# Attention: the last key quarter projected later, and two output-projection chunks between its transposed keys and its scores

## Chip, core and metric

One core of one Trainium2 chip. The metric is device time in microseconds. The kernel before took 1267.77 us (median of 3 runs, 1267.5 to 1268.72).

## What is computed

Two layers over 256 latent tokens (with a 256-token context in layer 0), each a half-step SwiGLU, a mixer and another half-step SwiGLU, with DeepNorm residuals. Layer 0's mixer is the neighbourhood attention that the change touches:

```
qkv = (hx @ w_qkv).reshape(B, S, 3, N_HEADS, HEAD_DIM)      # 16 heads of 64
q, k = apply_axial_rope(q), apply_axial_rope(k); v = qkv[:, :, 2]
s_win = einsum(q_rows, k_blk) * scale + bias   (window mask: -inf)
s_ctx = einsum(q_rows, k_c) * scale            (all 256 context keys)
p = softmax(concatenate([s_win, s_ctx]))
o = p_win @ v_blk + p_ctx @ v_c
y_lat = o.reshape(B, S, D) @ w_out
```

## The kernel before, in words

Everything is done in float32 accuracy by splitting each operand into a high and a low half: ScalarE (ACT) copies the high half, VectorE (DVE) subtracts to get the low half, and TensorE (PE) adds three products (`mmu`, L156: lines L160, L161 and L163, six matmuls of 128x512 for one *chunk*, that is one weight unit of two 128-row blocks against one token tile).

The attention stage works on these pieces.

- **Key quarters.** `kv_quarter(g)` (L879) projects keys and values of heads 4g to 4g+3: 16 chunks named wkv (4 token tiles by 4 weight units, `tile_panel`, L863). For each finished tile, `each` turns the keys (rope on DVE for the latent tiles; a plain copy on ACT, L887, for the two context tiles) and splits the values. Its `rest` (L895) is put off (`Late`): eight transposes in two groups of four write two PSUM banks named kT, from which ACT and DVE make kTh and kTl (L108, L109).
- **Query halves.** `q_half` (L908), 8 chunks wq and a late qT of the same kind.
- **Score pairs.** `scores(h, qt)` (L931): six matmuls S (L941) into two PSUM banks for the heads h and h+1 and one half of the queries. Then on DVE the bias is added (L945) and the maximum is taken (L947); on ACT the exponential (L949) reads the bank, and L951 scales it to the probabilities `pr`. There are 16 pairs in 32 steps.
- **Transposed probabilities.** `probs_T` (L960): four transposes into a bank PT, split into pTh on ACT and pTl on DVE. `values(h)` (L971): eight matmuls o, then osum on ACT (L984) and DVE (L985), and after two heads the split oT.
- **Output projection.** `last_filler` (L1007) loads the residual x and the gate and makes the chunks wo of `na_w_out` in the order of `order_late` (L494): three banks (t, n) = (0,0), (0,1), (1,0) first.
- **Bias.** `bias_pair` (L847) loads four small pieces per pair on the SP queue, POOL adds the window mask (L857). Four bias tiles serve two pairs, so that a pair's load waits until the pair two before it has added its own.

The PSUM has eight banks, `PB = {"mm": 3, "at": 3, "tp": 2}`. All transposes (PT, kT, qT, hT and the small mcT of `fold_cols`, L341) take the two tp banks in turn (`tpb`, L104). Score pairs take at banks, chunks and o take mm banks (`mmb`, L101), but a wo bank with t = 1 is an at bank too.

PE's order is the order of the Python program; ACT, DVE, SP and POOL are ordered by a scheduler with priorities. The loop of L1033 to L1060 sets PE's order: at step i it places the score pair (even i), some chunks of a generator `fill`, the PT of step i-2 and the o of step i-3. How many chunks a step gets is `rate`: R0 for steps 0 to 7, R1 for 8 to 15, R2 for 16 to 23 and R3 after that. `fill` yields key quarters 1 and 2, query half 1 and key quarter 3 (L1001). A `while` (L1038) makes chunks in addition until the quarter that step i + AHEAD will read is complete. From step 24 on (L1048) `fill` is the output projection, of which the loop may use 9 chunks.

Of the kernel before, what the change touches and what calls it, by code (L numbers as in the profile page):

```python
# [20 lines left out]
NH = 16  # L21
# [21 lines left out]
NX_AT = 2  # L43
R0 = 2.4
R1 = 2.9
R2 = 1.9
R3 = 1.0
LN_LAG = (5, 5)
LT_LAG = (5, 5)
F0_LAG = (5, 5, 6, 7)  # L50
# [1 line left out]
ROPE_EARLY = 70  # L52
S_EARLY = 40
V_LAG = 1
AHEAD = 3
P_EARLY = 70
V_EARLY = 70
W_HI = 2
# [8 lines left out]
def backbone_kernel(  # L67
# [27 lines left out]
    def act(dt=F32, s="a"):  # L95
        return ap.tile([P, 512], dt, tag="act", name=nm(s))

    def bank(tag, s):
        return pp.tile([P, 512], F32, tag=tag, bufs=PB[tag], name=nm(s))

    def mmb(s="mm", t=0):  # L101
        return bank("at" if t % 2 else "mm", s)

    def tpb(s="tp"):  # L104
        return bank("tp", s)

    def split(src, hi, lo):
        a = nc.scalar.activation(hi, src, AF.Copy)  # L108
        return a, nc.vector.tensor_tensor(out=lo, in0=src, in1=hi.bitcast(F32), op=ALU.subtract)  # L109
# [344 lines left out]
    def run(gen):  # L454
        for _ in gen:
            pass
# [37 lines left out]
    def order_late(nu, halved=False):  # L494


        e = nu - 1
        banks = ((0, 0), (0, 1), (1, 0))
        o = [(t, n, u) for t, n in banks for u in range(e - 1)] + [(t, n, e - 1) for t, n in banks]
        if halved:  # L500
            o += [(t, n, (e, i)) for i in range(UK) for t, n in banks]
        else:
            o += [(t, n, e) for t, n in banks]
        return o + [(1, 1, u) for u in range(nu)]
# [167 lines left out]
    steps = ((0, 1), (1, 1), (2, 2), (4, 2), (6, 2))  # L672
# [80 lines left out]
    def new_x(l, i, pool=None):  # L753
        lnr = ln_rows(l, i, pool)
        for t in range(2):
            for h in range(2):
                nc.vector.tensor_tensor(out=xt[t][h], in0=xt[t][h], in1=lnr[0][h], op=ALU.mult)
                nc.vector.tensor_tensor(out=xt[t][h], in0=xt[t][h], in1=lnr[1][h], op=ALU.add)
# [35 lines left out]
    def lhs_T(tl):  # L794
        def f(k, t):
            s = (k % 2) * 256 + t * P
            g = tl[k // 2]
            hi, lo = g.get() if isinstance(g, Late) else g
            return hi[:, s:s + P], lo[:, s:s + P]
        return f  # L800
# [23 lines left out]
    def rtile(n):  # L824
        if n == 256:
            return hp.tile([P, n], F32, tag="kr", bufs=8, name=nm("kr"))
        return sp.tile([P, n], F32, tag="s2", bufs=S2, name=nm("qr"))

    def roped(src, t, which, nh):
        n = nh * HD  # L830
        C = rope[:, t, 2 * which, :]
        S = rope[:, t, 2 * which + 1, :].rearrange("p (a b e) -> p a b e", a=2, b=2)
        r1 = rtile(n)
        r2 = sp.tile([P, n], F32, tag="tmp", bufs=3, name=nm("r2"))
        nc.vector.tensor_tensor(out=r1.rearrange("p (h d) -> p h d", h=nh), in0=src.rearrange("p (h d) -> p h d", h=nh),
                                in1=C.unsqueeze(1).to_broadcast([P, nh, HD]), op=ALU.mult)
        bv = src.rearrange("p (h a b e) -> p h a b e", h=nh, a=2, b=2)
        rv = r2.rearrange("p (h a b e) -> p h a b e", h=nh, a=2, b=2)
        for b in range(2):
            nc.vector.tensor_tensor(out=rv[:, :, :, b, :], in0=bv[:, :, :, 1 - b, :],  # L840
                                    in1=S[:, :, b, :].unsqueeze(1).to_broadcast([P, nh, 2, 16]), op=ALU.mult)
        nc.vector.tensor_tensor(out=r1, in0=r1, in1=r2, op=ALU.add)
        return r1
# [19 lines left out]
    def tile_panel(c0, c1, hl, s, each):  # L863

        units = []
        for t, hT in enumerate(hl):
            bk = mmb(s)
            for u in range(KU):
                if t == 0:
                    units.append(wpair(w_qkv, u, c0, c1, s))  # L870
                hi, lo = units[u]
                mmu(bk, [(*hsl(hT, UK * u + i), hi[:, i], lo[:, i]) for i in range(UK)], u == 0, u == KU - 1)
                if u == KU - 1:
                    with tc.high_priority(offset=ROPE_EARLY):
                        each(t, bk)
                yield
                tick()

    def kv_quarter(g, res):  # L879
        krs, v = [], []  # L880

        def each(t, bk):
            if t < 2:
                krs.append(roped(bk[:, 0:256], t, 1, 4))
            else:
                r1 = rtile(256)
                nc.scalar.activation(r1, bk[:, 0:256], AF.Copy)  # L887
                krs.append(r1)
            v.append(act(F32R, "v"))
            z = v[t].rearrange("p (h s d) -> p h s d", h=4, s=2)  # L890
            split(bk[:, 256:512].rearrange("p (h d) -> p h d", h=4), z[:, :, 0], z[:, :, 1])

        yield from tile_panel(D + g * 256, 2 * D + g * 256, [hTs[t] for t in range(4)], "wkv", each)

        def rest():  # L895
            kT = []
            for j in range(2):
                ps = tpb("kT")
                for t in range(4):
                    nc.tensor.transpose(ps[:, t * P:(t + 1) * P], krs[t][:, j * P:(j + 1) * P], ident)  # L900
                hi, lo = act(F32R, "kTh"), act(F32R, "kTl")
                split(ps, hi, lo)
                kT.append((hi, lo))
            return kT

        res.append((Late(1, rest), v))
# [22 lines left out]
    KV, Q = [], []  # L929
# [71 lines left out]
    def filler():  # L1001
        yield from kv_quarter(1, KV)
        yield from kv_quarter(2, KV)
        yield from q_half(1, Q)
        yield from kv_quarter(3, KV)

    def last_filler():  # L1007
        with tc.issue_after(bias_dma[-1].ins):
            for t in range(2):
                for h in range(2):  # L1010
                    xt[t][h] = act(F32, "x")
                    sync.dma_start(xt[t][h], xscr[t * P:(t + 1) * P, h * 512:(h + 1) * 512])
            gen, nh, lt = sub_end(na_w_out[0], lhs_T(oT), KC, 0, 1, 5, 1.0, (0, 6), "wo", order_late(KU, True))
        box.extend([nh, lt])
        yield from gen

    box = []
    fill = filler()
    rate = [R0] * 8 + [R1] * 8 + [R2] * 8 + [R3] * 12
    credit = 0.0  # L1020
    steps = [(h + i, qt) for h in range(0, NH, 2) for qt in range(2) for i in range(2)]
    prs = {}
    LAG = A_LAG
    fin = None

    def fill_some(n):
        for _ in range(n):
            if next(fill, 0) == 0:
                break

    fill_some(A_PRE)
    for i in range(len(steps) + LAG + V_LAG):
        if i == NX_AT:  # L1033
            new_x(0, 0, s2t)
            for t in range(2):
                for h in range(2):
                    sync.dma_start(xscr[t * P:(t + 1) * P, h * 512:(h + 1) * 512], xt[t][h])
        while i + AHEAD < len(steps) and len(KV) <= steps[i + AHEAD][0] // 4:  # L1038
            fill_some(1)
        if i < len(steps) and i % 2 == 0:  # L1040
            with tc.high_priority(offset=S_EARLY):
                prs[i], prs[i + 1] = scores(*steps[i])
            if i % 2 == 0 and i + 2 < len(steps):
                bias_pair(*steps[i + 2])
        credit += rate[min(i, len(rate) - 1)]
        n = int(credit)
        credit -= n
        if i >= 24 and fin is None:  # L1048
            run(fill)
            fin = last_filler()  # L1050
            fill = islice(fin, 10)
        fill_some((n + 1) // 2)
        if i == len(steps) + LAG - 1:
            run(fill)
        if 0 <= i - LAG < len(steps):
            with tc.high_priority(offset=P_EARLY):
                probs_T(*steps[i - LAG], prs.pop(i - LAG))
        fill_some(n // 2)
        j = i - LAG - V_LAG
        if j >= 0 and steps[j][1] == 1:  # L1060
            with tc.high_priority(offset=V_EARLY):
                values(steps[j][0])
# [80 lines left out]
    g, hTs, later = sub_end(sc_w_out[0], lhs_T(yT), KC, 1, 1, 5, 1.0, (1, 6), "wo", order_late(KU))  # L1143
# [57 lines left out]
```

## Time and profile before

| | |
|---|---|
| median of 3 runs | 1267.77 us |
| the profiled execution | 1267.5 us |
| its span, first to last instruction | 1265.7 us |
| mean granted TensorE clock | 0.998 |
| PE busy | 1241.6 us |
| DVE busy | 955.1 us |
| ACT busy | 591.4 us |

The span is the time from the first to the last instruction of the profiled execution; 1.8 us lie around it. An idle time of an engine is put down to what released it, in brackets behind the instruction that ended it. A busy PE says only that matmuls were in flight: they overlap, so the spacing between starts is the better measure of what a matmul costs.

### The profile page before, as it was taken

To read this page: it belongs to the slowest core of one execution; us is meant where nothing else is said; L and a number is where in the kernel's file an instruction comes from. 1 tells how busy PE (TensorE), PEld (TensorE's weight loads), DVE (VectorE), ACT (ScalarE), POOL (GpSimd) and SP (SyncE) were. 2 spreads that over 40 slices of the span, in tenths; PEclk is the share of its full clock that TensorE was granted. 3 is DMA by queue.
4 is the path that set the end of the run, shared out by engine and by line. 5 is a ranking of instruction groups with operands and counts; after the bars stand their busy time and mean duration, and the time that the engine had idled before them with its cause. 6 is when DMAs were issued, how large, how long until landed. Compare 5 with 4: busy or idle time off the path is not lost.

```text
span 1265.7 us, 17259 instructions
## 1 busy us (share of the span) xinstructions
PE 1241.6 (98%) x5890; PEld 1004.0 (79%) x5890; DVE 955.1 (75%) x1685; ACT 591.4 (47%) x1152; POOL 41.6 (3%) x71
## 2 busy tenths in 40 slices
PE   6999999999999999999999999999999999999997
PEld 4787778787778878777888788888788887888786
DVE  4698987588888867889888646988546788877546
ACT  2433132312326556687655535655435644655431
POOL 0000000000001111111000000000000000000000
PEclk9999999999999999999999999999999999999999
DMA  9977679597872744464899745898645764886641
GB/s 283 299 243 233 179 235 300 168 304 232 294 237 84 209 100 86 99 135 135 261 323 335 233 145 175 268 330 278 223 149 168 238 211 134 257 288 186 218 159 57
DMA packets 202776, 268.59 MB, mean 212 GB/s; under 512 B 30090, under 2 KB 149362, under 8 KB 202688
## 3 DMA queue, kind: packets, MB, share of 16 engines
q1 hardware_dynamic: 202652, 267.48, 67.4%
q8 instruction: 46, 0.75, 0.2%
q14 instruction: 42, 0.34, 0.1%
q10 hardware_dynamic: 36, 0.02, 0.0%
HBM read 265.27 MB, written 2.17 MB: 211 GB/s over the span
## 4 chain that ended last, share of the span: by engine, by line
PE 90%; DVE 4%; DMA 3%; ACT 2%; issue 1%; POOL 0%; SPq 0%; DVEq 0%; ACTq 0%; POOLq 0%
PE f L655 19%; PE w L160 17%; PE w L163 17%; PE w L161 17%; PE wkv L160 2%; PE wkv L161 2%; PE wkv L163 2%; PE wc L160 2%; PE wc L163 2%; PE wc L161 2%; DMA bias<-in_na_rpb_dram 2%; PE gT L473 1%; PE ada L315 1%; PE S L941 1%; PE hT L407 1%; PE ada L595 1%
## 5 line engine op out<-in xcount | busy, mean ns | idle before, releaser
L206 ACT ACTIVATE w1h<-w1r 128x512 fp32r<-128x512 f32 (+1 forms) x352 | 200.5, 620 | 186.7 <-PE w L163 63.6
L209 DVE TENSOR_TENSOR w1l<-w1r,w1h 128x512 fp32r<-128x512 f32 (+1 forms) x352 | 222.6, 678 | 52.9 <-ACT w1h L206 51.4
L160 PE MATMUL w<-w1h,hTh 128*128 128x512 f32 x528 | 209.5, 397 | 0.9 <-ACT hTh L108 0.9
L161 PE MATMUL w<-w1l,hTh 128*128 128x512 f32 x528 | 206.0, 390 | 0.2 <-DVE w1l L209 0.2
L284 DVE SCALAR_TENSOR_TENSOR acc<-ar,cst,acc 128x512 f32<-128x512 f32 x266 | 185.4, 744 | 16.0 <-DMA ar<-in_ada_w_dram 15.9
L160 PE MATMUL w<-w2h,gh 128*128 128x512 f32 (+1 forms) x446 | 173.6, 390 | 0.3 <-ACT gh L108 0.3
L161 PE MATMUL w<-w2l,gh 128*128 128x512 f32 (+1 forms) x446 | 172.1, 386 | 0.0
L209 DVE TENSOR_TENSOR w2l<-w2r,w2h 128x512 fp32r<-128x512 f32 x176 | 114.1, 686 | 72.7 <-ACT w2h L206 72.0
L206 ACT ACTIVATE w2h<-w2r 128x512 fp32r<-128x512 f32 x176 | 101.5, 624 | 143.8 <-PE w L163 107.6
L163 PE MATMUL w<-w1h,hTl 128*128 128x512 f32 x528 | 163.3, 390 | 0.3 <-DVE hTl L109 0.2
L655 PE MATMUL f<-h0h,w1h 128*128 128x512 f32 x352 | 137.9, 396 | 3.6 <-ACT w1h L206 2.6
L655 PE MATMUL f<-h0l,w1h 128*128 128x512 f32 x352 | 136.6, 392 | 0.0
L655 PE MATMUL f<-h0h,w1l 128*128 128x512 f32 x352 | 136.4, 392 | 0.0
L163 PE MATMUL w<-w2h,gl 128*128 128x512 f32 (+1 forms) x446 | 136.2, 386 | 0.0
L160 PEld LDWEIGHTS w<-w1h,hTh 128*128 128x128 f32 x528 | 99.2, 188 | 23.8 <-ACT hTh L108 1.7
L163 PEld LDWEIGHTS w<-w1h,hTl 128*128 128x128 f32 x528 | 98.9, 188 | 22.4 <-DVE hTl L109 1.5
L161 PEld LDWEIGHTS w<-w1l,hTh 128*128 128x128 f32 x528 | 99.3, 188 | 20.2 <-DVE w1l L209 0.6
L160 PEld LDWEIGHTS w<-w2h,gh 128*128 128x128 f32 x446 | 83.8, 188 | 19.9 <-issue 2.5
L163 PEld LDWEIGHTS w<-w2h,gl 128*128 128x128 f32 x446 | 83.3, 188 | 17.3 <-DVE gl L109 0.2
L161 PEld LDWEIGHTS w<-w2l,gh 128*128 128x128 f32 x446 | 83.8, 188 | 16.5
L655 PEld LDWEIGHTS f<-h0h,w1h 128*128 128x128 f32 x352 | 66.1, 189 | 21.8 <-issue 4.2
L655 PEld LDWEIGHTS f<-h0h,w1l 128*128 128x128 f32 x352 | 66.4, 189 | 13.8 <-issue 0.4
(180 smaller groups left out, 1699.5 us busy)
## 6 DMA issues: line engine op xcount, KB each, us to landing
w1r<-in_ffn_w_in_dram SPq DMA_DIRECT2D x340, 256.0 KB
ar<-in_ada_w_dram SPq DMA_DIRECT2D x128, 512.0 KB
w2r<-in_ffn_w_out_dram SPq DMA_DIRECT2D x88, 512.0 KB
ar<-in_ada_w_dram SPq DMA_DIRECT2D x32, 256.0 KB
wkvr<-in_na_w_qkv_dram SPq DMA_DIRECT2D x32, 256.0 KB
wcr<-in_sc_w_in_dram SPq DMA_DIRECT2D x32, 256.0 KB
wqr<-in_na_w_qkv_dram SPq DMA_DIRECT2D x8, 512.0 KB
bias<-in_na_rpb_dram SPq DMA_DIRECT2D x64, 64.0 KB
```

The lines of the kernel that those rows point to most:

```text
L160: nc.tensor.matmul(ps, lh, rh, start=first and i == 0, stop=False)
L161: nc.tensor.matmul(ps, lh, rl, start=False, stop=False)
L163: nc.tensor.matmul(ps, ll, rh, start=False, stop=last and i == n - 1)
L206: nc.scalar.activation(hi[:, a:a + m // W_HI], raw[:, a:a + m // W_HI], AF.Copy)
L209: nc.vector.tensor_tensor(out=lo[:, a:b], in0=raw[:, a:b], in1=hi[:, a:b].bitcast(F32), op=ALU.subtract)
L284: nc.vector.scalar_tensor_tensor(out=a, in0=src, scalar=sc, in1=a, op0=ALU.mult, op1=ALU.add)
L315: nc.tensor.matmul(ps[32 * j:32 * j + 32, :], ones, acc[i][h], start=True, stop=True)
L407: nc.tensor.transpose(ps[:, k * P:(k + 1) * P], z[h][:, k * P:(k + 1) * P], ident)
L473: nc.tensor.transpose(ps[:, j * 256 + i * P:j * 256 + (i + 1) * P], g[:, j * P:(j + 1) * P], ident)
L595: nc.tensor.matmul(ps[o:o + 32, 0:m], cst[:, a * kt + i, :], w[:, i, j, :], start=(a == 0 and i < 2), stop=(a == last and i >= kt - 2))
L655: nc.tensor.matmul(ps, w, hT0[k][part == 1], start=(k == part == 0), stop=(k == KC - 1 and part == 1))
L941: nc.tensor.matmul(banks[i], (qh, qh, ql)[f][ps, qs], (kh, kl, kh)[f][ps, :], start=f == 0, stop=f == 2)
```

## The change

- AHEAD goes from 3 to 1: a quarter has to be complete one step before it is read, not three. R2 goes from 1.9 to 1.45 and R3 from 1.0 to 0.8, so steps 16 to 23 place fewer chunks each, and so do the steps from 24 on.
- The switch to the output projection now stands ahead of the score pair of step 24. There the rest of quarter 3 is made, its kT is called for at once, and two wo chunks follow, and then the scores.
- The second kT bank of quarter 3 (and of that quarter alone) comes from the mm banks, not the tp banks.

```diff
-R2 = 1.9
-R3 = 1.0
+R2 = 1.45
+R3 = 0.8
...
-AHEAD = 3
+AHEAD = 1
...
             for j in range(2):
-                ps = tpb("kT")
+                ps = mmb("kT") if g == 3 and j else tpb("kT")
                 for t in range(4):
...
         while i + AHEAD < len(steps) and len(KV) <= steps[i + AHEAD][0] // 4:
             fill_some(1)
+        if fin is None and i + 1 < len(steps) and steps[i][0] == NH - 4:
+            run(fill)
+            fin = last_filler()
+            fill = islice(fin, 10)
+            KV[-1][0].get()
+            fill_some(2)
         if i < len(steps) and i % 2 == 0:
...
-        if i >= 24 and fin is None:
-            run(fill)
-            fin = last_filler()
-            fill = islice(fin, 10)
         fill_some((n + 1) // 2)
```

No instruction's work is added or taken away; the order moves. In the lists below a row is the line, the operation, and the result <- operands with the tiles' numbers.

**Place 1, PE, quarter 3's kT** (kT transposes of the turned keys kr, then S the first scores of the quarter, wo the output projection). Before:

```order
L966 MATMUL PT_5177<-ident,pr_5072 128x128 x4
L900 MATMUL kT_5184<-ident,kr_4812 128x128
L900 MATMUL kT_5184<-ident,kr_4879 128x128
L900 MATMUL kT_5184<-ident,kr_4957 128x128
L900 MATMUL kT_5184<-ident,kr_5090 128x128
L900 MATMUL kT_5193<-ident,kr_4812 128x128
L900 MATMUL kT_5193<-ident,kr_4879 128x128
L900 MATMUL kT_5193<-ident,kr_4957 128x128
L900 MATMUL kT_5193<-ident,kr_5090 128x128
L941 MATMUL S_5202<-kTh_5189,qTh_4778 128x512
```

and with the change:

```order
L966 MATMUL PT_5177<-ident,pr_5036 128x128 x4
L900 MATMUL kT_5184<-ident,kr_4845 128x128
L900 MATMUL kT_5184<-ident,kr_4965 128x128
L900 MATMUL kT_5184<-ident,kr_5067 128x128
L900 MATMUL kT_5184<-ident,kr_5170 128x128
L900 MATMUL kT_5193<-ident,kr_4845 128x128
L900 MATMUL kT_5193<-ident,kr_4965 128x128
L900 MATMUL kT_5193<-ident,kr_5067 128x128
L900 MATMUL kT_5193<-ident,kr_5170 128x128
L160 MATMUL wo_5227<-woh_5220,oT_4272 128x512
```

Two chunks (twelve matmuls) now stand between the transposes and S. The last two chunks of quarter 3 now stand right ahead of PT_5177, where before three PT, two o and a score pair stood between; kr_5170, the copy of its last tile, is read by the fourth transpose.

**Place 2, PE, quarter 1's kT**, some 88 us earlier. Before:

```order
L163 MATMUL wkv_4154<-wkvh_4156,hTl_3391 128x512 x2
L900 MATMUL kT_4170<-ident,kr_3946 128x128
L900 MATMUL kT_4170<-ident,kr_4030 128x128
L900 MATMUL kT_4170<-ident,kr_4112 128x128
L900 MATMUL kT_4170<-ident,kr_4149 128x128
L900 MATMUL kT_4179<-ident,kr_3946 128x128
L900 MATMUL kT_4179<-ident,kr_4030 128x128
L900 MATMUL kT_4179<-ident,kr_4112 128x128
L900 MATMUL kT_4179<-ident,kr_4149 128x128
L160 MATMUL wkv_4154<-wkvh_4189,hTh_3390 128x512
```

and with the change:

```order
L163 MATMUL wkv_4203<-wkvh_4205,hTl_3391 128x512 x2
L966 MATMUL PT_4221<-ident,pr_4087 128x128 x4
L900 MATMUL kT_4228<-ident,kr_3946 128x128
L900 MATMUL kT_4228<-ident,kr_4030 128x128
L900 MATMUL kT_4228<-ident,kr_4112 128x128
L900 MATMUL kT_4228<-ident,kr_4156 128x128
L900 MATMUL kT_4237<-ident,kr_3946 128x128
L900 MATMUL kT_4237<-ident,kr_4030 128x128
L900 MATMUL kT_4237<-ident,kr_4112 128x128
L900 MATMUL kT_4237<-ident,kr_4156 128x128
L160 MATMUL wkv_4203<-wkvh_4247,hTh_3390 128x512
```

A PT stands right ahead of this kT now, so three tp tiles follow one another with two banks.

**Place 3, ACT, from the third score pair of the last quarter to the fourth** (L949 the exponentials, L951 the scalings, L984 osum of a head's o, L206 weight halves woh). Before:

```order
L949 ACTIVATE pr_5405,mx_5403<-S_5394,mx_5403 128x512
L949 ACTIVATE pr_5412,mx_5410<-S_5395,mx_5410 128x512
L108 ACTIVATE pT_5385<-PT_5444 128x4x128
L951 ACTIVATE pr_5405<-pr_5405,mx_5403 128x512
L984 ACTIVATE osum_5460<-o_5451 64x256
L951 ACTIVATE pr_5412<-pr_5412,mx_5410 128x512
L206 ACTIVATE woh_5531<-wor_5530 128x512
L206 ACTIVATE woh_5567<-wor_5566 128x512 x2
L949 ACTIVATE pr_5474,mx_5472<-S_5463,mx_5472 128x512
```

and with the change:

```order
L949 ACTIVATE pr_5418,mx_5416<-S_5407,mx_5416 128x512
L108 ACTIVATE pT_5398<-PT_5465 128x4x128
L951 ACTIVATE pr_5418<-pr_5418,mx_5416 128x512
L984 ACTIVATE osum_5481<-o_5472 64x256
L949 ACTIVATE pr_5425,mx_5423<-S_5408,mx_5423 128x512
L951 ACTIVATE pr_5425<-pr_5425,mx_5423 128x512
L949 ACTIVATE pr_5495,mx_5493<-S_5484,mx_5493 128x512
```

The second exponential of the third pair now stands behind osum of o_5472, the product that PE makes right ahead of the fourth pair (S_5484 and S_5485). The weight halves that stood ahead of the last pair's first exponential have moved ahead of the rows shown. On PE the wo bank (1,0), which is an at bank, begins ahead of the third pair with the change, and behind it before. On SP the four loads of x and the two of the gate (256 KB each) come one score pair earlier among the bias loads, and ahead of the last pair's bias loads there now stand the last wo unit (512 KB) and the next stage's first weight unit (2 x 256 KB). POOL's order is the same.

## Rows read from the trace of the kernel before

**Rows 1.** The page: span, and busy time, share and instructions of each engine
```profile
span 1265.7 us, 17259 instructions
...
PE 1241.6 (98%) x5890; PEld 1004.0 (79%) x5890; DVE 955.1 (75%) x1685; ACT 591.4 (47%) x1152; POOL 41.6 (3%) x71
```
**Rows 2.** PE timeline, 520 to 590: start, us, engine, line, form [idle before <- releaser]
```profile
520.06 0.66 PE L966 MATMUL PT<-ident,pr 128*128 128x128 f32 x4 [0.16 <-DVE qTl L109]
...
547.30 0.39 PE L978 MATMUL o<-pT,v 128*128 128x256 f32 x1 [0.74 <-ACT pT L108]
548.25 0.39 PE L979 MATMUL o<-pT,v 128*128 128x256 f32 x1 [0.56 <-DVE pT L109]
...
555.79 0.66 PE L900 MATMUL kT<-ident,kr 128*128 128x128 f32 x4 [1.61 <-DVE pT L109]
...
573.62 0.38 PE L979 MATMUL o<-pT,v 128*128 128x256 f32 x1 [0.58 <-DVE pT L109]
...
574.65 0.50 PE L941 MATMUL S<-kTh,qTh 64*128 64x512 f32 x2
...
584.17 0.39 PE L979 MATMUL o<-pT,v 128*128 128x256 f32 x1 [0.42 <-DVE pT L109]
```
**Rows 3.** Windows of 1 us: length, busy per engine (instructions), PE clock, DMA share, GB/s
```profile
550.00:551.00 1.00, 1.00 (x6) 0.44 (x3) 0.81 (x3) 1.00 (x3) 0.00 (x0) 0.50 0.80 96
...
552.00:553.00 1.00, 1.00 (x7) 1.00 (x6) 0.73 (x2) 0.83 (x2) 0.40 (x1) 0.50 0.67 153
...
555.00:556.00 1.00, 0.21 (x2) 0.21 (x3) 0.96 (x2) 1.00 (x4) 0.73 (x1) 1.00 0.68 82
```
**Rows 4.** The chain of waits, in order of time, 540 to 600: start, us, what
```profile
547.78 7.23 DMA bias<-in_na_rpb_dram
...
562.20 7.53 DMA bias<-in_na_rpb_dram
...
571.35 0.43 DVE S L945
```
**Rows 5.** PE timeline, 541 to 544: a chunk, four transposes, a score pair
```profile
541.20 0.40 PE L160 MATMUL wkv<-wkvh,hTh 128*128 128x512 f32 x1
...
542.59 0.60 PE L966 MATMUL PT<-ident,pr 128*128 128x128 f32 x4
543.12 0.50 PE L941 MATMUL S<-kTh,qTh 64*128 64x512 f32 x2
...
544.01 0.51 PE L160 MATMUL wkv<-wkvh,hTh 128*128 128x512 f32 x1
```
**Rows 6.** PE timeline, quarter 1's kT and the next PT
```profile
465.32 1.03 PE L900 MATMUL kT<-ident,kr 128*128 128x128 f32 x8
466.11 0.48 PE L160 MATMUL wkv<-wkvh,hTh 128*128 128x512 f32 x1
...
469.25 0.66 PE L966 MATMUL PT<-ident,pr 128*128 128x128 f32 x4 [0.15 <-DVE kTl L109]
```
**Rows 7.** Timelines of PE, ACT and DVE: one PT and its two copies
```profile
560.88 0.60 PE L966 MATMUL PT<-ident,pr 128*128 128x128 f32 x4
...
561.51 0.60 ACT L108 ACTIVATE pT<-PT 128x512 fp32r<-128x512 f32 x1 [0.56 <-PE PT L966]
...
562.15 0.69 DVE L109 TENSOR_TENSOR pT<-PT,pT 128x512 fp32r<-128x512 f32 x1 [0.33 <-ACT pT L108]
```
**Rows 8.** DVE timeline: what a score pair asks of DVE
```profile
456.69 0.76 DVE L945 TENSOR_TENSOR S<-S,bias 128x256 f32<-128x256 f32 x2 [1.02 <-PE S L941]
457.36 1.28 DVE L947 TENSOR_REDUCE mx<-S 128x1 f32<-128x512 f32 x2
```
**Rows 9.** ACT timeline: osum right behind o, then an exponential
```profile
553.34 0.38 ACT L984 ACTIVATE osum<-o 64x256 f32<-64x256 f32 x1 [0.51 <-PE o L979]
553.74 0.69 ACT L949 ACTIVATE pr<-S,mx 128x512 f32<-128x512 f32 x1
```
**Rows 10.** SP timeline: issues of the x loads and of bias loads
```profile
558.65 1.84 SPq L1012 DMA_DIRECT2D x<-xscr  x4
...
561.53 5.71 SPq L853 DMA_DIRECT2D bias<-in_na_rpb_dram  x8
```

## The prediction

> **What bounds the kernel now.** The page comes first: PE is busy 1241.6 of 1265.7 us [rows 1], so a gain must come out of the 24 us in which it is idle, or out of matmuls that run slowly. PE's timeline then shows where that is within attention. From 470 to 545 us there is one wait, of 0.16 us [rows 2]. Then, between 546 and 556, come three: 0.74 and 0.56 us for the copies of a PT, and 1.61 us at the second half of quarter 3's kT [rows 2]. The reader should see why: in this stretch no chunk stands between PT, o, kT and S, since quarter 3 is already complete and the output projection may not start before step 24. Two more waits of the kind, 0.58 and 0.42 us, follow at 573 and 584 [rows 2]. The windows show a second loss: in the three windows from 550 to 553 the granted clock is 0.50, the 1.2 GHz level [rows 3]. Ahead of it PE had idled for 0.74 + 0.56 = 1.30 us. Behind the longer idle of 1.61 us the clock is 1.00 [rows 3], so an idle of this length may cost clock or not.
>
> The chain of waits tells something else about the same place: between 547 and 571 it runs largely through two bias loads of 7.23 and 7.53 us, into a bias addition at 571.35 [rows 4]. That is kept for a rival.
>
> **The change, part by part.** All sums are against the profiled execution's own 1267.5 us; the median of the runs is 0.27 us above it.
>
> *What goes.* Five wkv chunks that stood ahead of the hole now stand in it, so each PT has a chunk of 1.39 us behind it [rows 5] before its o is due: the 1.30 us of idle go, and with them the half clock, 3 us at 0.50 = 1.50 us. The second kT bank is an mm bank now and waits for no PT: 1.61 us. The waits at 573 and 584 belong to the bias that came late; the x and gate loads, issued right ahead of the bias loads in the queue [rows 10], now come a pair earlier: up to 1.00 us, which I count in full here, and what takes the place of the second one is priced below. Sum 5.41 us. The S behind quarter 3's kT waits for two copies, about 2 us of work; two chunks, 2.8 us, cover them.
>
> *What is late next.* No row shows these waits in the new order, so each gets two bounds.
>
> 1. Quarter 1's kT. With AHEAD at 1 no chunks are forced there, and PT, kT, kT follow one another on two tp banks (place 2). This is the pattern that cost 1.61 us in quarter 3, and the new code exempts quarter 3 alone. Lower bound: a PT's copies take 0.63 + 0.64 + 0.69 = 1.96 us from its start [rows 7]; PT and the first kT, four transposes each, cover 2 x 0.40 of it (eight take 0.79 [rows 6]): 1.2 us. Upper: the score pair ends one chunk ahead of PT, and DVE has its two additions (0.76), two reductions (1.28) [rows 8] and two weight halves (0.69 each) to do before the PT copy (0.69): 4.1 us after the pair, where PE is there after 1.39 + 0.80: 1.9 us. I take the nearest row, 1.6.
> 2. Quarter 2's kT is followed by a PT after one chunk instead of two. Two chunks left a wait of 0.15 [rows 6]. Between 0 and one DVE copy (0.7); I take 0.15.
> 3. Quarter 3's fourth transpose reads the copy of a tile that PE finished just before (place 1, kr_5170). Between 0 and one exponential of 0.69 ahead of it on ACT [rows 9]; I take 0.3.
> 4. mcT takes a tp bank behind PT, S, PT: 1.96 us against 0.40 + 0.89 + 0.40 [rows 5, 6, 7] leaves 0.27. Between 0.2 and 1.0 (one exponential more); I take 0.3.
> 5. The last score pair. The at banks are three, one is held by wo (1,0) from the third pair on, so the fourth pair needs both exponentials of the third done. The second of them stands behind osum of the o that PE makes right ahead of the fourth pair (place 3). From the end of that o, osum takes 0.40 and the exponential 0.69 [rows 9]: PE stands 1.1 us. Lower 0 (no row excludes that the bank is free earlier), upper 1.7 (ACT one scaling behind). I take 1.1. Queued behind it on PE are all remaining chunks.
> 6. The tail. From the last pair at 574.65 to the last wait at 584.17 the chain S, exponential, PT, copies, o takes 9.5 us [rows 2]. With the change one chunk less (1.39) covers it, but three weight halves on ACT have gone from in front of its exponential (place 3). Between 0 and 1.4; I take 0.4.
>
> Sum 1.6 + 0.15 + 0.3 + 0.3 + 1.1 + 0.4 = 3.85 us. Bounds: 1.4 to 7.4.
>
> The other engines get no work. DVE (75% busy) and ACT (47%) [rows 1] do the same copies in a shorter stretch; where they are late is what the six items price. SP's last bias load now has 1 MB of weights ahead of it; its time from the pair two before it to its own addition was 571.35 - 562.20 = 9.2 us from issue [rows 4], against about 10 us between the two pairs on PE in the new order, so it is just covered, and what it costs if it is not is rival D.
>
> Net: 5.41 - 3.85 = 1.56 us off, **1265.9 us**. With the six items at their bounds: 1263.5 to 1269.5.
>
> *A rule of the skill.* The row shows half clock behind 1.30 us of idle and full clock behind 1.61 [rows 3]. The Trainium skill, "TensorE: Matmul & The Clock Gate", Part 1, The HAM clock gate, says that the low level is the default, that activity lifts it, and that the observation runs on its own, not from the kernel's events. By that rule item 1's idle among thin transposes could bring half clock to another stretch; by the row alone the price would be 1.50 us or nothing. My sum has nothing for it; with it the sum would be 0.06 us off, no change.
>
> **The rivals.**
>
> *B, the waits stay covered.* Items 2 to 6 come out near their lower bounds, since ACT is half idle over the kernel and its scheduler's order need not bind. For it: PE waits only 0.16 us in the 75 us ahead of the hole, though PT, kT and qT alternate there too. Against it: item 1 has a measured twin, and item 5 is an order on one queue. Time: 1267.5 - 5.41 + 1.4 = 1263.5 us.
>
> *C, slower.* The wait at quarter 1's kT reaches its upper bound because the DVE queue is full there, and it lowers the clock for three windows as at 550, and the last pair waits too. It decides where DVE is more than one copy late at PT_4221. Price: all items high (7.4) and 1.50 of clock, less 5.41: 3.5 us more, 1271.0; with half of the excess, 1268.8. For it: in DVE's new order the pair's seven additions, reductions, reciprocals and weight halves stand ahead of the copy. Against: the 0.15 us that the same kT's next PT waited [rows 6] shows a DVE that is hardly late there.
>
> *D, the change moves rows, but not the end.* The chunks do move (place 1), but the pace from 547 on is set by bias load, mask, addition, softmax [rows 4], and PE's waits are only what it shows. Then what goes at 556 returns at the last pair, and the time stays: 1267.5 us, within 0.5. For it: the chain runs through the loads. Against: the loads at 562.20 were late because of the x loads ahead of them [rows 10].
>
> **How the numbers follow.** Forecast A (1264.6 to 1267.4 as its own range, 1265.9 likeliest) 0.48; B 0.30; C 0.12; D 0.10. A measurement of this kernel can tell about 0.2%, 2.5 us, from no change: faster is below 1265.2, slower above 1270.3. B lies below, and 0.13 of A: faster 0.43. The rest of A (0.35), D (0.10) and 0.02 of C: same 0.47. The rest of C: slower 0.10. The range reaches from a little below B's time to C at half its excess: 1262.9 to 1269.0.
>
> **What would show it.** Right: no half clock between 545 and 560; no wait at quarter 3's second kT; a wait of 1.2 to 1.9 us at quarter 1's second kT, released by DVE's pT copy; a wait of about 1 us at the last S, released by ACT's exponential (L949); mcT and the last PT a few tenths late. Wrong: PE waits in attention below 2 us in all (B); half clock at 470 (C); a bias addition that is released by POOL and has the last S behind it (D).

## The result, and the profile of the changed kernel

The changed kernel is slower. Beside the kernel before, run on the same chip, it took 1272.38 us (median of 11 runs, 1270.42 to 1276.62) against 1268.06 (median of 11, 1267.34 to 1270.12): ratio 1.0027, 95% interval 1.0017 to 1.0037. By the ratio that is 3.4 us more; the two medians lie 4.3 us apart. The prediction had 1265.9 us and a range up to 1269.0. The profiled execution took 1272.38 us, of which the span is 1270.6.

The page answers to [rows 1]: PE is busy 1.5 us longer, and the span is 4.9 us longer. The other engines' times differ by about 1 us, so no work was added; PE stands more, and part of its work runs slower.

```profile
span 1270.6 us, 17261 instructions
...
PE 1243.1 (98%) x5890; PEld 1004.3 (79%) x5890; DVE 956.4 (75%) x1685; ACT 591.5 (47%) x1152; POOL 40.7 (3%) x71
```

First what the change was made for. The window over the old hole, 546 to 556, shows 10.00 us of PE work at clock 1.00 (columns as in [rows 3]). Before, the same ten microseconds held waits of 0.74, 0.56 and 1.61 us [rows 2] and three windows at half clock (granted 0.50, the 1.2 GHz level) [rows 3].

```profile
546.00:556.00 10.00, 10.00 (x58) 8.18 (x58) 7.89 (x18) 8.28 (x21) 1.77 (x2) 1.00 0.50 85
```

So the hole is gone. PE's timeline shows where the time went instead; these are all its waits of 0.5 us and more from the first score pair to the first hT (the transposes that open the next stage). The number in the bracket is the idle time, the second column is the length of the instruction.

```profile
471.37 0.79 PE L900 MATMUL kT<-ident,kr 128*128 128x128 f32 x4 [2.07 <-DVE pT L109]
...
507.86 0.66 PE L966 MATMUL PT<-ident,pr 128*128 128x128 f32 x4 [1.48 <-DVE kTl L109]
...
526.82 0.65 PE L966 MATMUL PT<-ident,pr 128*128 128x128 f32 x4 [1.10 <-DVE qTl L109]
...
558.21 0.76 PE L900 MATMUL kT<-ident,kr 128*128 128x128 f32 x5 [0.65 <-ACT kr L887]
...
575.30 0.24 PE L350 MATMUL mcT<-ident,mrow 32*128 32x32 f32 x1 [0.55 <-DVE pT L109]
...
580.32 0.50 PE L941 MATMUL S<-kTh,qTh 64*128 64x512 f32 x1 [1.13 <-ACT pr L949]
...
588.05 0.63 PE L966 MATMUL PT<-ident,pr 128*128 128x128 f32 x4 [0.53 <-DVE pT L109]
```

The first three, 4.65 us, lie at quarter 1's second kT, at the PT behind quarter 2's kT and at the PT behind qT. In the kernel before the PT behind quarter 1's kT waited 0.15 us and the one behind qT 0.16 [rows 2, 6]; behind quarter 2's kT its timeline shows no wait. All three are for a tp bank: each starts just when DVE has emptied the bank that it overwrites. The last four, 2.86 us, stand where the kernel before had its hole and the waits of 0.58 and 0.42. The windows behind the first wait show the second loss: half clock, where the kernel before ran at full clock.

```profile
472.00:473.00 1.00, 1.00 (x4) 0.81 (x4) 0.65 (x1) 1.00 (x2) 0.00 (x0) 0.50 0.52 52
473.00:474.00 1.00, 1.00 (x4) 0.81 (x3) 0.69 (x1) 0.02 (x1) 0.00 (x0) 0.50 0.74 117
474.00:475.00 1.00, 1.00 (x5) 0.81 (x5) 0.00 (x0) 0.00 (x0) 0.73 (x1) 0.50 0.66 186
```

With the windows on both sides (0.88 and 0.92) that is 1.70 us of PE work lost. The kernel before had lost as much: its windows from 549 to 554 show 0.83, three times 0.50, and 0.97, which is 1.70 us too. Between these two profiles the half clock has moved, and cancels. Neither the 1.48 us of idle at 507 nor the 1.10 us at 526 was followed by half clock.

Measured from the first score pair to the first hT, attention takes 158.86 us (440.66 to 599.52) against 154.55 before (440.18 to 594.73), 4.3 us more.

DVE's timeline shows why the first wait is that long. The pT copy (470.65) frees the bank. Ahead of it DVE makes half of v, osum, the additions and maxima of the score pair that PE made one chunk ahead of the PT, a weight half for wkv and one for wq.

```profile
466.86 0.41 DVE L109 TENSOR_TENSOR v<-wkv,v 128x256 fp32r<-128x256 f32 x1
467.19 0.40 DVE L985 TENSOR_TENSOR osum<-o,osum 64x256 f32<-64x256 f32 x1
467.53 0.74 DVE L945 TENSOR_TENSOR S<-S,bias 128x256 f32<-128x256 f32 x2
468.19 1.27 DVE L947 TENSOR_REDUCE mx<-S 128x1 f32<-128x512 f32 x2
469.38 0.67 DVE L209 TENSOR_TENSOR wkvl<-wkvr,wkvh 128x512 fp32r<-128x512 f32 x1
...
470.06 0.66 DVE L209 TENSOR_TENSOR wql<-wqr,wqh 128x512 fp32r<-128x512 f32 x1
470.65 0.67 DVE L109 TENSOR_TENSOR pT<-PT,pT 128x512 fp32r<-128x512 f32 x1
```

The second wait has more behind it than one chunk less. In the kernel before two chunks stood between quarter 2's kT and the PT, and the bank that this PT takes was empty at 501.21, 0.83 us ahead of it (PE's rows, and DVE's copy of the first kT):

```profile
498.39 1.03 PE L900 MATMUL kT<-ident,kr 128*128 128x128 f32 x8
...
502.04 0.60 PE L966 MATMUL PT<-ident,pr 128*128 128x128 f32 x4
```
```profile
500.52 0.69 DVE L109 TENSOR_TENSOR kTl<-kT,kTh 128x512 fp32r<-128x512 f32 x1
```

With the change one chunk stands there, and a score pair now comes one chunk ahead of the kT. ACT works at that pair's exponentials and a scaling before it copies kTh, and DVE, which needs kTh, stands idle for it. The copy now ends 3.85 us after the first transpose of kT; before it took 2.82.

```profile
503.95 1.03 PE L900 MATMUL kT<-ident,kr 128*128 128x128 f32 x8
```
```profile
505.21 0.68 ACT L949 ACTIVATE pr<-S,mx 128x512 f32<-128x512 f32 x1
...
505.87 0.72 ACT L951 ACTIVATE pr<-pr,mx 128x512 f32<-128x512 f32 x1
506.49 0.59 ACT L108 ACTIVATE kTh<-kT 128x512 fp32r<-128x512 f32 x1
```
```profile
507.11 0.69 DVE L109 TENSOR_TENSOR kTl<-kT,kTh 128x512 fp32r<-128x512 f32 x1 [0.68 <-ACT kTh L108]
```

### The profile page after: what moved, and what is told of

Its sections match the earlier page's. It is cut to its first block, busy times and chain, and to the rows that moved or that the text cites. A ratio compares the mean times of both kernels' runs of the same rounds, so it can differ in the third digit from the quotient of the medians.

```text
span 1270.6 us, 17261 instructions
## 1 busy us (share of the span) xinstructions
PE 1243.1 (98%) x5890; PEld 1004.3 (79%) x5890; DVE 956.4 (75%) x1685; ACT 591.5 (47%) x1152; POOL 40.7 (3%) x71
## 4 chain that ended last, share of the span: by engine, by line
PE 89%; DVE 4%; ACT 3%; DMA 2%; issue 1%; POOL 0%; SPq 0%; DVEq 0%; ACTq 0%
PE w L160 17%; PE w L163 17%; PE f L655 17%; PE w L161 17%; PE wkv L160 2%; PE wkv L161 2%; PE wkv L163 2%; PE wc L160 2%; PE wc L163 2%; PE wc L161 2%; DMA ar<-in_ada_w_dram 1%; PE gT L473 1%; PE S L941 1%; PE ada L315 1%; PE wo L160 1%; PE wo L163 1%
## 5 line engine op out<-in xcount | busy, mean ns | idle before, releaser
L206 ACT ACTIVATE w1h<-w1r 128x512 fp32r<-128x512 f32 (+1 forms) x352 | 200.5, 620 | 185.0 <-PE w L163 65.1
L206 ACT ACTIVATE w2h<-w2r 128x512 fp32r<-128x512 f32 x176 | 101.6, 624 | 144.5 <-PE w L163 104.6
```

The lines of the kernel that those rows point to most:

```text
L206: nc.scalar.activation(hi[:, a:a + m // W_HI], raw[:, a:a + m // W_HI], AF.Copy)
```

## Experiments

**Theory T**: the loss is made in quarters 1 and 2 and at the second query half. The lower AHEAD and rates leave fewer chunks between one group of transposes and the next, and the two tp banks are then too few. The bank exception, which the change makes for quarter 3 alone, is missing there. **Rival L**: the late part is at fault, the new order of the last pairs. **Theory D** came in with the first runs: the bias loads of the late pairs are a floor. Ratios are to the kernel before on the same chip, whose median moved between 1268.06 and 1269.96 us from one comparison to the next; so only ratios are compared. Lengths of attention are of one profile each, from first pair to first hT.

### 1. AHEAD 3 for the early quarters

```
-        while i + AHEAD < len(steps) and len(KV) <= steps[i + AHEAD][0] // 4:
+        ah = AHEAD if len(KV) > 2 else 3
+        while i + ah < len(steps) and len(KV) <= steps[i + ah][0] // 4:
```

> The changed kernel with AHEAD 3 again for quarters 1 and 2, and 1 for quarter 3 alone; the two chunks, the mm bank and the lower rates stay. Theory T (the loss is made in quarters 1 and 2 and at the second query half, by fewer chunks between a transpose group and the next one): the waits of 2.07 us (471), 1.48 (507) and 1.10 (526) shrink to 0.2 each at most and the half clock at 472 to 475 goes, 4.3 + 1.5 us; but quarter 3 has no chunk left for two of the hole's o, which gives 0.6 to 2.8 us back (waits like the 0.74 and 0.56 of before, with or without half clock). Time 1267.2 to 1269.5. Rival L (the late part is the cause: the order of the last four pairs, with waits of 0.65, 0.55, 1.13 and 0.53): early waits go too, but the time stays at 1271 or more, since what PE gains early it waits for at the last pairs.

Measured: 1.0006 (0.9993 to 1.0018), attention 155.81 us, no half clock. Of the early waits 0.16 and 0.22 us are left, as T has it. The ratio lies in T's range (1267.2 to 1269.5 us is 0.999 to 1.001 of 1268.06), but not for T's reason: what takes part of the gain back is a wait of 2.54 us at the last-but-one pair, which neither theory had. PE's row, and DVE's behind it:

```profile
577.16 0.66 PE L966 MATMUL PT<-ident,pr 128*128 128x128 f32 x4 [2.54 <-DVE pT L109]
```
```profile
574.74 0.43 DVE L945 TENSOR_TENSOR S<-S,bias 128x256 f32<-128x256 f32 x1 [2.00 <-POOL bias L857]
```

DVE waits for the bias with its additions, and the pT copies are queued behind them. SP's queue shows why the bias is late: the x and gate loads, 6.6 us of issuing, stand ahead of it.

```profile
559.88 4.05 SPq L1012 DMA_DIRECT2D x<-xscr  x4
564.57 1.92 SPq L331 DMA_DIRECT2D gate<-scr  x2
566.59 2.74 SPq L853 DMA_DIRECT2D bias<-in_na_rpb_dram  x4
```

This is the mechanism of the prediction's rival D, at another pair.

### 2. The mm bank in all quarters

```
-                ps = mmb("kT") if g == 3 and j else tpb("kT")
+                ps = mmb("kT") if j else tpb("kT")
```

> The changed kernel with its mm bank for the second half of kT in quarters 1, 2 and 3, not in 3 alone; the order on PE is the same. If the wait of 2.07 us at quarter 1's second kT is for a tp bank alone: it goes, the half clock behind it goes too, and the time falls by about 3.6 us to 1268.8; the waits at 507 and 526 stay at 1.5 and 1.1. If DVE's lateness is the cause and the bank only where it shows: the next instruction that needs DVE (the o behind, or the next PT) waits instead for 1 to 2 us, and the time stays within 1 us of 1272.4.

Measured: 0.9979 (0.9968 to 0.9989); PE's order is that of the changed kernel. Attention takes 152.68 us, 6.2 us less than in the changed kernel. The kernel was measured once more, beside those of experiments 9, 11 and 12 (run 10): 0.9982 (0.9970 to 0.9994), as expected. The eight transposes of quarter 1 now follow one another without a wait, the wait at 507 is gone as well, and no window of attention is at half clock. Of the early waits only the one behind qT, whose banks are unchanged, is left.

```profile
469.08 1.04 PE L900 MATMUL kT<-ident,kr 128*128 128x128 f32 x8
...
502.75 0.60 PE L966 MATMUL PT<-ident,pr 128*128 128x128 f32 x4
...
521.09 0.66 PE L966 MATMUL PT<-ident,pr 128*128 128x128 f32 x4 [0.52 <-DVE qTl L109]
```
```profile
503.65 0.69 DVE L109 TENSOR_TENSOR kTl<-kT,kTh 128x512 fp32r<-128x512 f32 x1 [0.69 <-ACT kTh L108]
```

The PT behind quarter 2's kT (502.75) now starts ahead of the first copy of kT (503.65): it takes the tp bank that kT no longer uses. DVE's pT copy at quarter 1 comes no sooner after its PT than in the changed kernel (471.02 for a PT at 468.65; there 470.65 for 468.27). So DVE is as late as it was, and it is the bank that decides whether PE has to stand for it. What goes is 2.07, 1.48, the half clock's 1.70 and 0.58 at qT, 5.8 of the 6.2 us. The expectation was too small, since it left the wait at 507 in place.

> The kernel with the mm bank in all quarters once more, beside the others on one chip: 0.997 to 0.999 of before. Theory T as for the first run of it: no wait at 471, none at 507, no half clock in attention.

### 3. AHEAD alone

```
-AHEAD = 3
+AHEAD = 1
```
in the kernel before.

> The kernel before with AHEAD 1 and nothing else. Theory T: the three early waits (2.07, 1.48, 1.10) and the half clock at 472 are there as in the changed kernel, +5.8 us; the hole at 546 to 553 is filled, -2.8 us; the wait of 1.6 us at quarter 3's second kT stays. Time 1270 to 1272 against 1268.1. Rival L (AHEAD harmless, the new end at fault): the hole's 2.8 us are won without a loss, 1265.3 to 1267.

Measured: 1.0033 (1.0020 to 1.0046), attention 157.42 us. The early waits are there, 2.07, 1.49 and 0.53 us, though none of the new late order and none of the lower rates is in this kernel; so L fails, and AHEAD alone is enough for the first two. Late in the stage the expectation was off: quarter 3's wait of 1.61 us turned into 0.78 and 0.58 at its two kT and 1.11 and 0.23 at the scores behind them, and half clock followed there (559 to 563, 1.71 us lost). Quarter 1 ran at full clock this time, behind the same idle time as in the changed kernel. PE's row, and windows behind it:

```profile
471.17 0.66 PE L900 MATMUL kT<-ident,kr 128*128 128x128 f32 x4 [2.07 <-DVE pT L109]
```
```profile
472.00:473.00 1.00, 1.00 (x6) 0.83 (x5) 0.60 (x2) 0.82 (x2) 0.00 (x0) 1.00 0.44 44
473.00:474.00 1.00, 1.00 (x9) 0.96 (x9) 0.54 (x1) 0.00 (x0) 0.00 (x0) 1.00 0.71 99
```

### 4. AHEAD 3 early, and chunks spread to the end

Experiment 1 with `R2 = 1.0`, `R3 = 1.0`.

> As the first of these, with R2 1.0 and R3 1.0, so that quarter 3 has a chunk left for every step up to 23: early order of the kernel before, late order of the changed one. Theory T: no early wait over 0.2 us, no half clock, no hole; what is left are the late waits, 0.65, 0.55, 1.13 and 0.53 and perhaps 0.5 at each of three o that now stand right behind a PT: 1265.5 to 1267.5, under both kernels. Rival L: 1270 or more.

Measured: 1.0026 (1.0014 to 1.0039): a miss. The early part is as in the kernel before, and of the hole one wait of 0.35 us is left; but at the last-but-one pair PE waits 4.06 us and at the last one 2.31. Half clock comes with both (575 to 582, beginning while PE still waits, and 589 to 595).

```profile
576.11 0.79 PE L161 MATMUL wo<-wol,oT 128*128 128x512 f32 x1 [4.06 <-DVE wol L209]
...
587.88 0.50 PE L160 MATMUL wo<-woh,oT 128*128 128x512 f32 x1 [2.31 <-ACT oT L108]
```
```profile
573.84 0.43 DVE L945 TENSOR_TENSOR S<-S,bias 128x256 f32<-128x256 f32 x1 [1.99 <-POOL bias L857]
```

The late bias holds DVE up again, and the weight half that PE needs is queued behind it.

### 5 and 6. Without the two chunks, and without quarter 3's mm bank

Run 5 takes `fill_some(2)` out of the changed kernel; run 6 takes its `mmb` out (`ps = tpb("kT")`).

> The changed kernel without the two output-projection chunks ahead of the first score pair of heads 12 and 13 (they are made later, in the tail); all else as changed. Theory T: the S behind quarter 3's kT waits for its copies, 1.3 us in all (1.11 + 0.23 where AHEAD 1 was tried alone). Theory D (the loads of bias for the last-but-one pair are a floor: they were ready 22 to 27 us after the third pair of quarter 2's last heads began, 24.9 in the changed kernel, where PE took 22.9 from that pair to the one that needs them): with 2.8 us less work between, DVE waits for POOL's bias at that pair and PE stands 1 to 3 us behind it. T alone gives 1272.4 + 1.3 - 0.5 (tail better covered) = 1273.2; T and D 1274 to 1276; if neither holds, the two chunks were of no use: 1271.5 to 1272.5.

> The changed kernel with quarter 3's second kT in a tp bank again; order on PE as changed. Theory T: PE waits there for the copies of the PT ahead, 0.6 to 1.6 us beyond the 0.65 that it waits in the changed kernel, and the half clock may come with it (1.5 us more): 1273 to 1275. Rival: the transposes wait for kr (ACT) anyway, so the bank is worth nothing: 1272.4.

Measured: 1.0042 (1.0026 to 1.0058) and 1.0039 (1.0025 to 1.0052). Both lie above the changed kernel's 1.0027, but the intervals overlap; what these parts are worth is read from waits. Without the chunks the scores wait for their keys, 0.48 and 0.33 us; with the tp bank the second kT waits 1.16 us:

```profile
558.59 0.50 PE L941 MATMUL S<-kTh,qTh 64*128 64x512 f32 x2 [0.48 <-ACT kTh L108]
559.42 0.50 PE L941 MATMUL S<-kTl,qTh 64*128 64x512 f32 x2 [0.33 <-DVE kTl L109]
```
```profile
557.05 0.66 PE L900 MATMUL kT<-ident,kr 128*128 128x128 f32 x4 [1.16 <-DVE pT L109]
```

So the two chunks and quarter 3's mm bank work in the way the prediction said, though on waits of 0.8 and 1.2 us, not of 2 and 1.61; in the total time neither is resolved. D's wait did not show in run 5: POOL had the bias of the last-but-one pair ready at 571.2, ahead of the addition at 574.12. Half clock from 560 to 563 stretched the pairs there; whether the bias would have been late without it was not tried.

### 7. The old rates

Experiment 2 with `R2 = 1.9`, `R3 = 1.0`.

> The kernel with the mm bank in all quarters (measured at 0.9979 of before) with R2 1.9 and R3 1.0 again, so that two chunks fewer stand between the third pair ahead of quarter 3 and the last pairs. Theory D: the bias loads do not come sooner, so PE waits at the last-but-one pair (DVE's addition released by POOL) by 1.5 to 3 us: 1268.5 to 1270. Rival: chunks made earlier cost nothing in a stretch where PE is full: 1266.5 to 1267.

Measured: 1.0012 (1.0001 to 1.0022), 4.2 us over experiment 2. The size is D's, the place is not: no addition waits for POOL. With these rates a wo chunk stands ahead of the PT behind the last-but-one pair, and it waits for its low half, then another one, behind the last pair, for oT:

```profile
571.21 0.51 PE L161 MATMUL wo<-wol,oT 128*128 128x512 f32 x1 [1.17 <-DVE wol L209]
...
582.70 0.60 PE L160 MATMUL wo<-woh,oT 128*128 128x512 f32 x1 [2.57 <-ACT oT L108]
```

Half clock follows both (573 to 576 and 583 to 586). So the lower rates of the change are worth about 4 us with the bank in all quarters.

### 8 and 9. More mm banks

Experiment 2 with `ps = mmb("qT") if j else tpb("qT")`; run 8 also with `ps = mmb("mcT")`.

> The kernel with the mm bank in all quarters, and the second half of qT and mcT from mm banks too; order as there. Bank theory: the waits of 0.52 us (PT behind qT) and 0.55 (mcT) go, and since loads of bias then had no slack left (575.0 ready, addition at 575.16 in the changed kernel), half of it may come back: 1265.6 to 1266.7. Rival: mm banks are short there, and a chunk waits instead: 1266.7 to 1268.

> The kernel with the mm bank in all quarters (0.9979) and the second half of qT from an mm bank too; mcT stays in its tp bank (with both moved, an o waited 3.79 us and the time was 1.001). If the qT bank does what the kT bank did: the wait of 0.52 us behind qT goes and nothing else comes, ratio to before 0.9970 to 0.9980. If the 3.79 us came from the qT bank and not from mcT's: they are there again, ratio 1.000 to 1.001.

Measured: 1.0010 (1.0000 to 1.0020) with both, above both ranges, and 0.9973 (0.9961 to 0.9984) with qT alone, as expected. The wait behind qT goes in both. With mcT in an mm bank, an o waits 3.79 us, and half clock follows (575 to 579, 1.70 us lost). PE's row, and one of DVE's:

```profile
574.71 0.36 PE L978 MATMUL o<-pT,v 128*128 128x256 f32 x1 [3.79 <-ACT pr L951]
```
```profile
574.38 0.18 DVE L352 COPY gcol<-mcT 128x32 f32<-128x32 f32 x1
```

Two of the three mm banks hold wo there, so mcT and the o share the third. The copy that empties it ends at 574.56, just ahead of the o, and stands behind three weight halves on DVE. The view names ACT as the releaser; the bank fits better. Run 9, which differs in mcT's bank alone, has no such wait, so mcT's bank is the cause; the way it acts is argued from the order of the rows. Run 9 has the lowest ratio of this study, 3.4 us under the kernel before and by the two ratios some 7 under the changed one; its interval overlaps that of experiment 2, so what the qT bank adds is shown by the wait and not by the time.

### 11. AHEAD 3 early, x loads behind the bias

Experiment 1 with the four x loads issued in the loop at i = 26, behind `bias_pair(*steps[28])`, not in `last_filler`.

> AHEAD 3 for quarters 1 and 2 as in the first experiment, and the four x loads issued behind the bias loads of the last-but-one pair, not two pairs earlier. Theory D (x and gate loads on SP's queue hold up that bias by some 5 us, and DVE, then PE, wait for it: 2.00 and 2.54 us there): both waits go, and the time falls by 2 to 2.5 us, ratio 0.998 to 0.999 (1.0006 with the x loads early). Rival: the bias is late by its own landing time (6.4 us on the chain there), and the time stays at 1.000 to 1.001; or the x loads become late at the residual (DVE L372), which gives it back.

Measured: 0.9999 (0.9989 to 1.0010), where experiment 1 had 1.0006. On SP's queue the bias is issued 3.4 us earlier, and this is what is left of PE's wait:

```profile
563.19 2.87 SPq L853 DMA_DIRECT2D bias<-in_na_rpb_dram  x4
566.79 3.10 SPq L1053 DMA_DIRECT2D x<-xscr  x4
```
```profile
575.14 0.66 PE L966 MATMUL PT<-ident,pr 128*128 128x128 f32 x4 [0.29 <-DVE pT L109]
```

The 2.54 us wait is 0.29 now: the queue order was its cause. Part comes back: the last pair's bias is 0.51 us late, and a wo chunk waits 0.71 us for oT. The time missed D's range of 0.998 to 0.999; it agrees in sign only, and the intervals overlap.

### 12. The bank alone

The kernel before with `ps = mmb("kT") if j else tpb("kT")`.

> The kernel before with the mm bank for the second half of kT in all quarters, and nothing else. Bank theory: the 1.61 us at quarter 3's second kT go; the hole (0.74 and 0.56 us, with or without half clock) stays: ratio 0.998 to 0.999. Theory D: the bias of the last-but-one pair was late already in the kernel before (addition at 571.35 against a pair at 568.07), so what is won at kT is waited for there: ratio 0.9995 to 1.0005.

Measured: 0.9994 (0.9983 to 1.0005). The wait of 1.61 us at quarter 3's second kT goes, but its first kT waits 0.41 us and the S behind them now waits for its copies, 1.18 and 0.98, and D is not needed to explain that nothing clear of noise is won:

```profile
552.77 1.09 PE L900 MATMUL kT<-ident,kr 128*128 128x128 f32 x8 [0.41 <-DVE pT L109]
...
555.04 0.50 PE L941 MATMUL S<-kTh,qTh 64*128 64x512 f32 x2 [1.18 <-ACT kTh L108]
...
556.53 0.50 PE L941 MATMUL S<-kTl,qTh 64*128 64x512 f32 x2 [0.98 <-DVE kTl L109]
```

The hole of this kernel stood again, 0.75 and 0.57 us, and this time no half clock followed it:

```profile
550.00:551.00 1.00, 1.00 (x10) 0.69 (x7) 0.99 (x4) 1.00 (x3) 0.00 (x0) 1.00 0.72 82
```

So neither the bank alone (0.9994) nor AHEAD alone (1.0033) gains; bank in all quarters, late quarter 3, two chunks and lower rates together do (0.9979). The rates are needed for it (experiment 7); whether the two chunks are was not tried there.

## Why the prediction was wrong

**What goes: right.** The hole, its half clock, the wait at quarter 3's second kT and those at 573 and 584 are gone, 5.41 us, or 5.61 with the half clock at its measured 1.70.

**Item 1, quarter 1's kT: place and releaser right, size and consequence wrong.** 2.07 us, above the upper bound of 1.9. The bound counted two additions, two maxima, two weight halves and the copy, and all of these are there; it left out an osum and a v half that DVE still had to do when the pair ended (0.4 each). And half clock followed, for which the sum had nothing: 1.70 us in the profiled execution.

**Item 2, the PT behind quarter 2's kT: this is the step that failed most clearly.** Priced 0.15 us [0 to 0.7], measured 1.48. The 0.15 us of [rows 6] is the wait behind quarter 1's kT. Quarter 2's own group had no wait in the kernel before, and 0.83 us to spare. The prediction took one group's wait for another's and left it as it was, though a chunk of cover, 1.39 us [rows 5], goes; and it did not ask what ACT has to do ahead of the copies, which end 1.03 us later after the transposes than before. The three make 1.39 + 1.03 - 0.83 = 1.6 us, near what was measured.

**What was not priced: the PT behind qT.** Here too one of two chunks goes, and 0.16 us [rows 2] became 1.10. The row was used only to show that the stretch is quiet. Being above zero, it said that there was no slack. The 1.10 is one profile's: in experiments 2, 3, 5 and 6, with one chunk as well, the wait is 0.51 to 0.53, and 0.66 in run 10. What makes it longer in the changed kernel's profile was not followed up.

**Items 3 to 6: right in place, somewhat low.** 0.65 for 0.3, 0.55 for 0.3, 1.13 for 1.1 (released by the exponential L949, as said), 0.53 and 0.14 for 0.4.

The items, with the 1.10 at qT, come to 7.65 us, not 3.85. With the 1.70 of half clock, less the 0.31 that stood around quarter 1's kT and behind qT before, they take 9.0 us against the 5.6 that go: 3.4 us more. Attention is longer by 4.3; 0.9 us of that are not assigned.

**The rivals.** What came is nearest to C: quarter 1's wait over its bound, half clock behind it, the last pair waiting, and 3.5 us more by the price given there. That its number fits is in part luck: C had items 3 to 6 at their upper bounds, 4.8 us where 3.0 came, and nothing for qT, and it had 0.7 for item 2. Its "half of the excess, 1268.8", near which the range ends, does not come out of its own terms either: half of 3.5 us on 1267.5 is 1269.2. C got a chance of 0.12, because the 0.15 us of [rows 6] was read as a DVE that is hardly late. B was excluded. D did not act in the changed kernel, but its loads were in time with no slack (POOL ready at 575.01, DVE's addition at 575.16), and experiments 1 and 11 show that it is the next limit: a version that won the early waits back in another way ran into it.

**The half clock.** In the profiles here, 2.01 to 2.07 us of idle at the same place of the program, quarter 1's second kT, was followed by half clock in the changed kernel and in run 5, and by full clock in runs 3 and 6. The hole's 1.3 us was followed by half clock in the kernel before and by full clock in run 12; in run 1 even 2.54 us at 577 was followed by full clock (the window from 577 to 578 shows 1.00). The Trainium skill, "TensorE: Matmul & The Clock Gate", Part 1, The HAM clock gate, says that the observation of activity is free-running and does not start anew with a kernel. By that, idle time of this length buys a chance of half clock and not a fixed price, and these profiles agree, though none shows the observation itself. The sum should have had 1.70 us times a chance for item 1's wait, not zero.

## What to carry over

A small wait in a profile is not a sign of quiet but of slack used up: at qT, one chunk less of cover turned 0.16 us into 0.5 to 1.1. And the row of one group says little about the next group of its kind: read that group's own rows, and what the engines that empty its buffer have to do just before. When a setting changes the spacing of work in the whole stage, check each group that shares the scarce buffer, not only the one that the change names; here one more bank for every quarter turned 1.0027 into 0.9979. And a load that lands just in time can take the next gain back (2.54 us of wait in experiment 1, 0.29 with its queue in another order), so look at its queue too.

## What was not expected of the hardware

The same wait at the same place is followed by half clock in some executions and not in others (2.07 us with and without). Where it came in the two kernels compared, it cost 1.70 us in each, and more behind the longer waits of run 4. So one profile of such a kernel does not show what it takes on the average. In the changed kernel's 11 runs the time goes with the mean granted clock of the run: the three at 0.999 took 1270.42 to 1271.13 us, the two at 0.996 took 1275.0 and 1276.62. So at least part of the scatter of some 6 us goes with the clock; what makes the clock differ from run to run was not tried. The kernel before scattered as widely in the later comparisons.
